# One decoder layer on one core: an eleventh early place for the weights, a fused first-values projection, another token order and a rebuilt end

## The chip, the core and the metric

The kernel runs on one core of a Trainium2 chip. The metric is the device time of one execution in microseconds (us); smaller is better. In the text PE is the matmul engine (TensorE), ScalarE is ACT in the rows, VectorE is DVE, GpSimd is POOL and SyncE is SP; SP issues almost all DMAs. PEld in a row is PE's loading of the stationary operand, which runs beside its matmuls.

## The reference, cut to what matters

One layer of a decoder over 256 tokens of 1024 float32 values: two attention branches (a sliding-window one and a forgetting one) from one input projection, sigmoid gates, an output projection and a layer norm, then a router that picks 4 of 32 experts per token, the experts, and a second layer norm.

```python
proj = h @ w_in[layer]
qa, ka, va, qf, kf, vf, fl, ga, gf = jnp.split(proj, split_points, axis=-1)
...
mix = jax.nn.sigmoid(ga) * ya + jax.nn.sigmoid(gf) * yf
h = _layer_norm(DEEPNORM_ALPHA * h + mix @ w_out[layer], ln1_g[layer], ln1_b[layer])
m = _moe(h, w_router[layer], b_router[layer], w_gate_up[layer], b_gate_up[layer], w_down[layer], b_down[layer])
h = _layer_norm(DEEPNORM_ALPHA * h + m, ln2_g[layer], ln2_b[layer])
```

An expert is `act(xb @ w_gate_up[e]) @ w_down[e]`: 8 MB of weights in its first half and 4 MB in its second, some 400 MB in all, each read once.

## The kernel before, in words

The order of the instructions on each engine is the order of the program: the scheduling is manual, and an engine that waits keeps all that stands behind it waiting. Tiles come from pools with a number of buffers; a new tile of a name takes the buffer of the tile that many allocations before it, and its first writer waits until every reader of that older tile is done. A wait is on semaphores that the framework places.

**The prologue.** The first part computes the input projection in twenty blocks. Each block of `w_in` is loaded by SP, split by `split` (L108 to L111) into a rounded part and a rest (ScalarE writes `hi`, VectorE then writes `lo`), and multiplied with the split, transposed input in three matmuls per chunk: `projT` (L304 to L315) gives transposed results, `projN` (L317 to L330) plain ones. Both write PSUM tiles of the pool `pj`, which has two buffers; `turn_x` uses it too. A block's split stands some blocks ahead of its projection in program order. The first values and forget logits (block 1, 136 columns) go through `projN` at L345, right after the first key projection and the split of block 3; their results leave PSUM through `evac`, which takes ScalarE and VectorE in turn. The attention scores follow, with the remaining blocks in between.

**The middle.** `split_u` (L474 to L492) splits half rows of the two branch projections and of `w_out` for 32 steps u. Steps 5 to 8 and the even ones from 24 have places of their own; all others take a tile `w_r` from five buffers. The splits of steps 0 to 5 stand ahead of the passes that use them. The passes (L570 to L591) run the steps 0 to 12, then 14, 13 and 15; after passes 0 to 4 stand the splits 9 to 13, after the pass of step 9 and every one behind it the splits 14 to 20. Where a pass ends a branch, VectorE multiplies the gate into the result (L582 or L584, L585), ScalarE rounds it (L586) and VectorE forms the rest (L566); the output projection (L614) reads these. The layer norm, the router and the one-hot matrices follow for two halves of 128 tokens, with filler matmuls (`busy`) that keep PE running while VectorE picks the experts (L669 to L680 and the list behind them).

**The weights of the experts.** `load_next` (L142 to L160) loads them in a fixed order, item by item: for each expert the four quarters of its first matrix (2 MB each) and the two halves of its second, which come one expert later. The first 32 items go to small places of 2 MB, a ring of ten that the prologue also uses for its own tiles; an eleventh place, `extra`, is opened after the prologue and used for item 10 alone. From item 32 on, five big places of 4 MB take two items at once. `refill` (L162 to L180) is called after the matmuls that use a place, and lets SP issue the next load; SP waits until the place is free. The first load of the big places follows when the small ones are closed.

**The experts.** Each expert e runs `up_proj` (64 half passes on PE), the combine of expert e-2 into four PSUM accumulators (L900), `scatter`, the gather of later tokens, `swiglu` and `down` of expert e-1. `up_proj` has eight chunks of 128 input channels; a chunk can start when its piece of the weights has landed. Items of the last experts are loaded in pieces: halves from item 166 on, quarters for the three big tiles ahead of the last, and six pieces for the last tile (L129 to L137).

**The end.** `last_down` (L1043 to L1048) runs the last second matrix in two column halves k. `last_combine` (L1050 to L1060) copies a half twice out of PSUM, so that each token half t has it on its own 64 rows, multiplies it into the accumulators and calls `stats`. Then VectorE, ScalarE and GpSimd scale and shift the four quarters (L1071 to L1093), and SP and ScalarE store them.

Of the kernel before, what the change touches and what calls it, by code (L numbers as in the profile page):

```python
# [35 lines left out]
def layer(tc, x, w_in, b_forget, sink, w_proj_swa, w_proj_fox, w_out, ln1_g, ln1_b, w_router, b_router,  # L36
# [9 lines left out]
    with ExitStack() as ctx:  # L46
# [5 lines left out]
        slots = {i: small.enter_context(tc.tile_pool(name=f"slot{i}", bufs=1, side="right")) for i in reversed(slot_of[1:] + slot_of[:1])}  # L52
# [19 lines left out]
        alpha_i = per.tile([P, P], F32, name="alpha_i")  # L72
# [48 lines left out]
        def fetch(kind, e, q, r, n=1, steps=1):  # L121
# [3 lines left out]
            dst, k = r.rearrange("p (c n) -> p c n", c=m * n), m * n // steps  # L125
            for i in range(0, m * n, k):
                sp.dma_start(dst[:, i:i + k], src[:, i:i + k])
# [69 lines left out]
        with tc.tile_pool(name="hd", bufs=1) as hd:  # L197
# [25 lines left out]
            with ExitStack() as at_ctx:  # L223
# [12 lines left out]
                dve.tensor_scalar(alpha_i, ident, ALPHA, None, op0=OP.mult)  # L236
# [45 lines left out]
                def split_in(i, parts=(0, 1)):  # L282
# [3 lines left out]
                    if i not in hls:  # L286
                        tl = slot_tile(1 + i % 3, F32R)
                        hls[i] = [tl[:, 8 * n * k:8 * n * (k + 1)].rearrange("p (c n) -> p c n", n=n) for k in (0, 1)]
                    for q in parts:
                        cs = slice(4 * q, 4 * q + 4)  # L290
                        for k, r in enumerate(raws[i]):
# [5 lines left out]
                            else:  # L297
                                split(*[a[:, cs, 128 * k:128 * k + m] for a in hls[i]], r[:, cs])
# [46 lines left out]
                projN(1, [(v[:, :, 0:128], 0, 128), (fl, 128, 136)])  # L345
# [128 lines left out]
                def split_u(u):  # L474
# [11 lines left out]
                    else:  # L486
                        w_r = p2.tile([P, 2, 512], F32R, name="w_r", bufs=5)
# [5 lines left out]
                for i in range(10):  # L493
# [12 lines left out]
                    if i == 0:  # L506
# [13 lines left out]
                        load_next(2)  # L520
                    if i == 7:
# [33 lines left out]
            wb = hd.tile([P, 8, NE], F32, name="wb")  # L555
            gnat = hd.tile([P, 2, 8], F32, name="gnat")
            sums = hd.tile([P, 2, NE], F32, name="sums")
# [41 lines left out]
            mv = hd.tile([P, 2, 2], F32, name="mv")  # L599
# [69 lines left out]
            def positions(t, pause=None):  # L669
# [3 lines left out]
                if pause:  # L673
                    pause(3)
# [446 lines left out]
```

## Time and profile before

| what | us |
|---|---|
| median of 3 runs | 1119.88 (1118.96 to 1120.91) |
| the profiled execution | 1119.41 |
| its span, first to last instruction | 1117.2 |
| PE busy | 1054.9 (94%) |
| VectorE busy | 378.3 (34%) |
| ScalarE busy | 211.3 (19%) |
| bytes read from HBM | 430.53 MB, 386 GB/s over the span |

The span leaves out what lies around it: the execution took 2.2 us more than its span. A matmul of float32 data shows as two instructions (half passes) in the counts: 64 for the 32 calls of `up_proj`. Busy shares are averages over stages that have different limits; what bounds one stage is read from the waits in it. PE's clock has two levels, 2.4 and 1.2 GHz; a granted clock of 1.00 in a row is the first, 0.50 the second, and what lies between is a mixture over the stretch.

### The profile page before, as it was taken

What the parts mean: (1) busy time and instruction counts of PE and PEld (TensorE: products, weight loads), DVE (VectorE), ACT (ScalarE), POOL (GpSimd) and SP (SyncE); (2) the same over time, 40 slices, a digit from 0 to 9 for tenths busy, and PEclk for the clock granted to TensorE, in tenths of its full rate; (3) what the DMA queues carried; (4) which work ended last, traced back from release to release, by engine and by line L of the source; (5) the groups of instructions that cost most, each with busy time, mean ns of one, the idle gap of its engine ahead of it and who ended that gap; (6) DMA issues with size and microseconds to landing.
All of it is one profiled execution on the core that took longest, in us unless ns stands there. A gap on an engine that the chain in (4) does not pass through costs nothing. (4 is left out here: it accounts for less than half of the span.)

```text
span 1117.2 us, 13432 instructions
## 1 busy us (share of the span) xinstructions
PE 1054.9 (94%) x5677; PEld 517.1 (46%) x5677; DVE 378.3 (34%) x821; ACT 211.3 (19%) x416; POOL 4.8 (0%) x14
## 2 busy tenths in 40 slices
PE   9999999999999999999999999999998988998895
PEld 8988897533333333333333343333433333333322
DVE  5577476432222224222222222222222222222223
ACT  5466464311111110000000110011000000000011
POOL 0000000000000000000000000000000000000001
PEclk9999999999999998999999999999999999999997
DMA  9754599999999999999999999999999999999993
GB/s 274 227 195 146 140 392 354 377 426 405 429 424 429 432 431 416 430 429 430 430 430 431 429 432 431 431 431 430 429 429 431 430 429 430 426 425 428 423 419 121
DMA packets 46406, 432.48 MB, mean 387 GB/s; under 512 B 5524, under 2 KB 26020, under 8 KB 29448
## 3 DMA queue, kind: packets, MB, share of 16 engines
q1 hardware_dynamic: 46144, 431.18, 93.5%
q8 instruction: 46, 0.75, 0.3%
q10 hardware_dynamic: 200, 0.41, 0.1%
q14 instruction: 16, 0.13, 0.0%
HBM read 430.53 MB, written 1.05 MB: 386 GB/s over the span
## 5 line engine op out<-in xcount | busy, mean ns | idle before, releaser
L851 PE MATMUL G<-ww,xTe 128*64 128x512 f32 x1664 | 368.2, 597 | 19.5 <-DMA ww<-in_w_gate_up_dram 19.1
L851 PEld LDWEIGHTS G<-ww,xTe 128*64 128x64 f32 x1664 | 119.3, 138 | 264.1 <-issue 227.3
L886 PE MATMUL X<-ww,aT 128*64 128x512 f32 x864 | 191.3, 595 | 0.5 <-DVE tb L871 0.3
L858 DVE COPY G_sb<-G 128x512 f32<-128x512 f32 x32 | 33.2, 1037 | 408.0 <-PE G L851 408.0
L860 ACT ACTIVATE G_sb<-G 128x512 f32<-128x512 f32 x32 | 33.8, 1055 | 422.3 <-PE G L851 422.3
L886 PEld LDWEIGHTS X<-ww,aT 128*64 128x64 f32 x864 | 59.6, 137 | 113.4 <-issue 107.6
L851 PE MATMUL G<-w,xTe 128*64 128x512 f32 x384 | 83.5, 593 | 0.6 <-POOL nth L773 0.6
L312 PE MATMUL pj<-w 128*128 128x256 f32 x232 | 66.7, 288 | 1.3 <-ACT w L110 0.8
L314 PE MATMUL pj<-w 128*128 128x256 f32 x232 | 65.7, 283 | 0.2 <-DVE w L111 0.2
L313 PE MATMUL pj<-w 128*128 128x256 f32 x232 | 65.6, 283 | 0.0
L809 PE MATMUL X<-OH,h_perm 128*128 128x128 f32 x480 | 63.0, 288 | 1.2 <-DVE h_perm L947 0.9
L900 PE MATMUL acc<-D_sb,GT 64*128 64x512 f32 x248 | 61.6, 615 | 0.7 <-DVE D_sb L893 0.7
L809 PEld LDWEIGHTS X<-OH,h_perm 128*128 128x128 f32 x480 | 60.1, 204 | 1.8 <-PE X L839 1.2
L868 PE MATMUL X<-ident,G_sb 128*128 128x128 f32 x256 | 40.0, 280 | 20.1 <-ACT xTe L822 12.0
L873 ACT ACTIVATE sg<-tb 128x256 f32<-128x256 f32 x64 | 26.7, 416 | 148.5 <-DVE tb L872 148.5
L851 PEld LDWEIGHTS G<-w,xTe 128*64 128x64 f32 x384 | 28.3, 137 | 53.6 <-issue 52.3
L893 DVE COPY D_sb<-X 128x256 f32<-128x256 f32 x31 | 13.2, 425 | 112.0 <-ACT D_sb L892 112.0
L111 DVE TENSOR_TENSOR w<-w 128x1024 fp32r<-128x1024 f32 (+2 forms) x50 | 46.3, 965 | 13.8 <-ACT w L110 13.8
L312 PEld LDWEIGHTS pj<-w 128*128 128x128 f32 x232 | 44.3, 191 | 3.9 <-issue 2.2
L871 DVE TENSOR_TENSOR tb<-X,bT 128x512 f32<-128x512 f32 x64 | 43.7, 683 | 4.1 <-PE X L868 4.1
L314 PEld LDWEIGHTS pj<-w 128*128 128x128 f32 x232 | 44.4, 191 | 0.4 <-DVE w L111 0.4
L313 PEld LDWEIGHTS pj<-w 128*128 128x128 f32 x232 | 44.4, 191 | 0.0
(263 smaller groups left out, 866.6 us busy)
## 6 DMA issues: line engine op xcount, KB each, us to landing
ww<-in_w_gate_up_dram SPq DMA_DIRECT2D x44, 4096.0 KB, 27.2
ww<-in_w_down_dram SPq DMA_DIRECT2D x23, 4096.0 KB, 28.2
w<-in_w_gate_up_dram SPq DMA_DIRECT2D x24, 2048.0 KB, 10.0
ww<-in_w_gate_up_dram SPq DMA_DIRECT2D x12, 2048.0 KB, 38.5
w<-in_w_down_dram SPq DMA_DIRECT2D x8, 2048.0 KB, 10.7
w<-in_w_in_dram SPq DMA_DIRECT2D x14, 1024.0 KB, 5.6
ww<-in_w_down_dram SPq DMA_DIRECT2D x6, 2048.0 KB, 39.7
ww<-in_w_gate_up_dram SPq DMA_DIRECT2D x8, 1024.0 KB, 28.3
```

The source lines that it names most:

```text
L111: dve.tensor_tensor(lo, src, hi.bitcast(F32), op=OP.subtract)
L312: pe.matmul(pt[:, j, :], hi[:, c, cs], xh[:, c, :], start=c == 0, stop=False)
L313: pe.matmul(pt[:, j, :], hi[:, c, cs], xl[:, c, :], start=False, stop=False)
L314: pe.matmul(pt[:, j, :], lo[:, c, cs], xh[:, c, :], start=False, stop=c == 7)
L809: pe.matmul(pt[:, c, :], h_perm[:, t, c0 + c, :], OH[:, t].rearrange("p a s -> p (a s)"), start=t == 0, stop=t == 1)
L851: pe.matmul(G[hf][64 * k:64 * k + 64, :], xT_e[:, c, :], w[:, c % 2, n0:n0 + 512], start=c == 0, stop=c == 7)
L858: dve.tensor_copy(dst, src)
L860: act.activation(dst, src, AF.Copy)
L868: pe.transpose(pt[:, c].rearrange("p k s -> p (k s)"), G_sb[:, c0 + c, :], ident)
L871: dve.tensor_tensor(tb, pt, bias[:, c0:c0 + 4, :, None].to_broadcast([P, 4, 2, CAP]), op=OP.add)
L886: pe.matmul(pt[64 * k:64 * k + 64, :], aT[:, c, :], w[:, c % 4, k * 512:(k + 1) * 512], start=c == 0, stop=c == 7)
L900: pe.matmul(acc[t][k], GT[r, t * P:(t + 1) * P], D_sb[r, :], start=first, stop=False)
```

## The change

It has six parts. The eleventh place is opened at the start, holds item 2 already during the attention (one more `load_next` at its step 3) and stays in the ring until the big places open; for its room the split weights `w_r` get four buffers instead of five, small tiles move from one pool to another, and the scaled identity `alpha_i` is made when it is used. The first values come from one wide matmul per chunk over `hi` and `lo` side by side plus a narrow one, for each token half in a PSUM tile of its own; a ScalarE copy and two VectorE additions sum the parts. In the token tail, the square root moves from `residual` into `shift`, the second half's transposes stand before the first gather, and fewer filler matmuls run. The loads of the experts are whole tiles except for the last three. In the last expert the combine and the scatter run ahead of the last two chunks. The end gets half-width combines, and three of its four output quarters are shifted and scaled by PE: a one-row matmul puts the bias into PSUM, a diagonal matmul adds the scaled values, ScalarE copies the result.

```diff
@@ places
-        slots = {i: ... for i in reversed(slot_of[1:] + slot_of[:1])}
+        slots = {i: ... for i in reversed(slot_of[9:] + slot_of[:9])}
+        extra_ctx = ExitStack()
+        extra = extra_ctx.enter_context(tc.tile_pool(name="extra", bufs=1, side="right"))
+        ring = [*slot_of[:2], None, *slot_of[2:]]
@@ load_next, refill
-                    r = extra.tile([P, 4096], F32, name="w") if i == 10 else slot_tile(slot_of[(i - (i > 10)) % 10])
+                    r = extra.tile([P, 4096], F32, name="w", tag="w") if i % 11 == 2 else slot_tile(ring[i % 11])
...
+                steps = {-6: (1, 1, 2), -4: (1, 1, 1, 1)}
...
-                    fetch(kind, slice(e, e + 1), q, r, 2, 4 if i + 8 >= len(items) else 2 if i + 26 >= len(items) else 1)
+                    fetch(kind, slice(e, e + 1), q, r, 2, *steps.get(i - len(items), (1,)))
...
-                if i - (11 if i < 21 else 10) >= used[0] - keep:
+                if i - (11 if nxt[0] < SMALL else 10) >= used[0] - keep:
@@ first values
-                projN(1, [(v[:, :, 0:128], 0, 128), (fl, 128, 136)])
+                for t in range(2):
+                    pt = pjp.tile([P, 2, 136], F32, name="pj")
+                    ts = slice(t * P, (t + 1) * P)
+                    for c in range(8):
+                        w = hls[1][2][:, c].rearrange("p k n -> p (k n)")
+                        pe.matmul(pt.rearrange("p k n -> p (k n)"), xh[:, c, ts], w, start=c == 0, stop=False)
+                        pe.matmul(pt[:, 0], xl[:, c, ts], hls[1][0][:, c, :], start=False, stop=c == 7)
+                    vl = at.tile([P, 136], F32, name="vl")
+                    act.activation(vl, pt[:, 1], AF.Copy)
+                    dve.tensor_tensor(v[:, t, 0:128], pt[:, 0, :128], vl[:, :128], op=OP.add)
+                    dve.tensor_tensor(fl[:, t], pt[:, 0, 128:], vl[:, 128:], op=OP.add)
@@ split weights, the extra load
-                        w_r = p2.tile([P, 2, 512], F32R, name="w_r", bufs=5)
+                        w_r = p2.tile([P, 2, 512], F32R, name="w_r", bufs=4)
...
+                    if i == 3:
+                        load_next()
@@ tokens
-                    act.activation(rs[:, t:t + 1], mv[:, t, 1:2], AF.Sqrt, bias=eps)
...
             def shift(t):
+                act.activation(rs[:, t:t + 1], mv[:, t, 1:2], AF.Sqrt, bias=eps)
...
-                    pause(3)
+                    pause(1)
...
+            shift(0)
             turn(0, 0, act)
             turn(0, 1, act)
-            shift(0)
...
-            gather0(0, 0)
             turn(1, 1, act)
             shift(1)
+            gather0(0, 0)
...
-            busy(idle, 2)
+            busy(idle, 1)
...
-            load_next()
@@ last expert
             def up_proj(xT_e, weights, beside=None):
...
+                    if c == 6 and beside:
+                        beside()
...
+                def others():
+                    if e > 1 and e != OVER + 1:
+                        combine(GTs[e - 2], Ds[e - 2], e == 2)
+                    if e == last:
+                        GTs[e] = scatter(OHg)
+                G_sb = up_proj(xTs[g][:, :, e % 2, :], lambda kind, q: where[kind, e, q], others if e == last else None)
                 refill(4, 2 if e == OVER else 0)
+                if e < last:
+                    others()
@@ end
             def last_combine(k):
...
+                for j in range(2):
+                    src, c = pt[k][64 * j:64 * j + 64], slice(256 * j, 256 * j + 256)
+                    act.activation(D2[:64, c], src, AF.Copy)
+                    dve.tensor_copy(D2[64:, c], src)
+                    for t in range(2):
+                        r = slice(64 * t, 64 * t + 64)
+                        pe.matmul(acc[t][k][:, c], GTs[last][r, t * P:(t + 1) * P], D2[r, c], start=False, stop=j > 0)
...
             last_down(1, 6, 7)
-            last_combine(0)
             last_down(1, 7, 8)
-            last_combine(1)
+            for k in range(2):
+                last_combine(k)
+                if k == 0:
+                    for t in range(2):
+                        stats(t, 0)
+            base = {}
+            for t, k in ((0, 0), (0, 1), (1, 0)):
+                base[t, k] = xp.tile([P, 512], F32, name="X") if t else gp.tile([P, 512], F32, name="G")
+                pe.matmul(base[t, k], ones[NE:NE + 1, :], rows[NE:NE + 1, cs[k]], start=True, stop=False)
...
+            def inverse(t):
+                dve.reciprocal(rs[:, t:t + 1], rs[:, t:t + 1])
+                diag[t] = mo.tile([P, P], F32, name="sg", bufs=2)
+                dve.tensor_scalar(diag[t], ident, rs[:, t:t + 1], None, op0=OP.mult)
+            def by_pe(t, k):
+                pe.matmul(base[t, k], diag[t], shifted[:, t, cs[k]], start=False, stop=True)
+                act.activation(y[:, t, cs[k]], base[t, k], AF.Copy)
+                store(t, k)
+            stats(0, 1)
+            scaled(0, 0)
+            inverse(0)
+            by_pe(0, 0)
+            stats(1, 1)
+            scaled(0, 1)
+            by_pe(0, 1)
+            inverse(1)
+            scaled(1, 0)
+            by_pe(1, 0)
+            scaled(1, 1)
+            dve.scalar_tensor_tensor(y[:, 1, cs[1]], shifted[:, 1, cs[1]], rs[:, 1:2], gb[:, 1, cs[1]],
+                                     op0=OP.mult, op1=OP.add)
+            store(1, 1)
```

`stats(t, k)` is one statistics operation on VectorE; for k = 1 an aggregation and ScalarE's square root follow. `scaled(t, k)` subtracts the mean and multiplies by the gain on VectorE, and `store` is an SP DMA. The four stores, and the loop of the last combine that is taken out, are left out of the diff above.

## Rows read from the trace of the kernel before

**Rows 1.** Windows: stretch, its length, PE, PEld, DVE, ACT, POOL, PEclk, DMA, GB/s.
```profile
269.00:272.00 3.00, 3.00 (x18) 1.00 (x16) 0.04 (x1) 0.00 (x0) 0.00 (x0) 1.00 0.76 240
272.00:430.00 158.00, 149.80 (x734) 58.33 (x730) 42.24 (x93) 19.30 (x37) 0.00 (x0) 1.00 1.01 429
810.00:960.00 150.00, 137.11 (x666) 52.57 (x662) 35.68 (x77) 13.27 (x25) 0.00 (x0) 0.98 1.00 430
965.00:1055.00 90.00, 83.79 (x416) 32.40 (x412) 22.39 (x47) 9.26 (x17) 0.00 (x0) 1.00 1.00 426
1060.00:1090.00 30.00, 27.27 (x126) 8.67 (x122) 6.43 (x15) 4.14 (x7) 0.00 (x0) 1.00 1.01 419
```
**Rows 2.** Timeline of SP, 194 to 205: start, length, instruction, count.
```profile
194.69 9.70 SPq L127 DMA_DIRECT2D w<-in_w_gate_up_dram  x2
```
**Rows 3.** Timelines of ACT, PE and DVE in the first 30 us.
```profile
12.16 0.23 PE L325 MATMUL pj<-w 128*128 128x136 f32 x1
...
17.48 0.33 PE L312 MATMUL pj<-w 128*128 128x256 f32 x1
...
29.80 0.36 PE L312 MATMUL pj<-w 128*128 128x256 f32 x1 [0.47 <-DVE w L97]
...
16.09 0.36 ACT L93 ACTIVATE w<-pj 128x256 f32<-128x256 f32 x1
...
20.15 1.67 ACT L110 ACTIVATE w<-w 128x512 fp32r<-128x512 f32 x3 [1.74 <-DMA w<-in_w_in_dram]
...
22.63 0.42 DVE L95 COPY v<-pj 128x256 f32<-128x256 f32 x1
```
**Rows 4.** Windows again, columns as in rows 1: two stretches at half clock.
```profile
661.00:664.40 3.40, 3.08 (x15) 2.91 (x14) 0.00 (x0) 0.71 (x2) 0.00 (x0) 0.51 1.03 443
1104.80:1117.00 12.20, 2.24 (x3) 0.50 (x2) 7.75 (x14) 1.37 (x3) 2.85 (x2) 0.50 0.23 86
```
**Rows 5.** Timelines of ACT, DVE and PE, 148 to 169, around the split weights.
```profile
152.55 0.63 ACT L110 ACTIVATE w_r<-w 128x512 fp32r<-128x512 f32 x1 [1.22 <-PE X L578]
...
156.75 0.63 ACT L110 ACTIVATE w_r<-w 128x512 fp32r<-128x512 f32 x1 [0.77 <-PE G L578]
...
158.02 0.68 DVE L584 TENSOR_TENSOR w<-w,G 128x512 f32<-128x512 f32 x1
...
167.75 0.50 PE L614 MATMUL acc<-w_r,w 128*128 128x512 f32 x1 [0.59 <-ACT w_r L110]
```
**Rows 6.** Timelines of PE and ACT, 189 to 201: the last tokens.
```profile
191.19 1.14 PE L684 MATMUL X<-OH,h_perm 128*128 128x128 f32 x8
...
193.52 1.08 PE L658 MATMUL acc<-wr,hT 128*128 128x32 f32 x8 [0.75 <-ACT hT L647]
...
197.75 2.02 PE L684 MATMUL X<-OH,h_perm 128*128 128x128 f32 x16 [0.17 <-DVE OH L679]
...
194.88 2.31 ACT L634 ACTIVATE h_perm<-x_sb,nm,rs 128x512 f32<-128x512 f32 x2
```
**Rows 7.** The chain that ended last, from the last expert's last chunk.
```profile
1078.52 1.94 PE G L851 x8
1080.46 1.92 PE acc L900 x8
...
1095.06 4.49 PE X L1047 x40
...
1104.10 2.96 PE acc L1058 x4
...
1113.41 0.75 DVE ww L1078
```
**Rows 8.** The page's costliest groups: busy us, mean ns, idle before.
```profile
L851 PE MATMUL G<-ww,xTe 128*64 128x512 f32 x1664 | 368.2, 597 | 19.5 <-DMA ww<-in_w_gate_up_dram 19.1
...
L858 DVE COPY G_sb<-G 128x512 f32<-128x512 f32 x32 | 33.2, 1037 | 408.0 <-PE G L851 408.0
```
**Rows 9.** Timeline of PE, 657 to 661: one-row matmuls.
```profile
657.02 3.79 PE L936 MATMUL X<-rows,ones 1*128 1x512 f32 x8
```

More of the change, by code (lines that the diff above doesn't have):

```diff
@@ L119, in layer, with fetch @@
         where, nxt, used, big = {}, [0], [0], []
-        def fetch(kind, e, q, r, n=1, steps=1):
+        def fetch(kind, e, q, r, n=1, *parts):
             src, m = (w_gate_up, 2) if kind == "G" else (w_down, 4)
             src = src[e].rearrange("a (p c) n -> p (a c) n", c=8)[:, m * q:m * q + m * n, :]
-            dst, k = r.rearrange("p (c n) -> p c n", c=m * n), m * n // steps
-            for i in range(0, m * n, k):
-                sp.dma_start(dst[:, i:i + k], src[:, i:i + k])
+            dst, i, unit = r.rearrange("p (c n) -> p c n", c=m * n), 0, m * n // max(sum(parts), 1)
+            for k in parts or (1,):
+                sp.dma_start(dst[:, i:i + k * unit], src[:, i:i + k * unit])
+                i += k * unit
         def fetch_last(r):
@@ L297, in split_in @@
                             else:
-                                split(*[a[:, cs, 128 * k:128 * k + m] for a in hls[i]], r[:, cs])
+                                split(*[a[:, cs, 128 * k:128 * k + m] for a in hls[i][:2]], r[:, cs])
                     if 1 in parts and i != 11:
@@ L970, in layer @@
                     OH = onehot(g + 1)
-                G_sb = up_proj(xTs[g][:, :, e % 2, :], lambda kind, q: where[kind, e, q])
+                def others():
[4 more added lines that the diff above has]
+                G_sb = up_proj(xTs[g][:, :, e % 2, :], lambda kind, q: where[kind, e, q], others if e == last else None)
                 refill(4, 2 if e == OVER else 0)
-                if e > 1 and e != OVER + 1:
-                    combine(GTs[e - 2], Ds[e - 2], e == 2)
+                if e < last:
+                    others()
                 if e == NORM:
@@ L1001, in layer @@
                     act.dma_start(rows[NE:], ln2_b)
-                GTs[e] = scatter(OHg)
+                if e < last:
+                    GTs[e] = scatter(OHg)
                 if 2 * (g + 1) <= last:
@@ L1052, in last_combine, with stats, scaled, store @@
                 D2 = mo.tile([P, 512], F32, name="tb", bufs=2)
-                for r in (slice(0, 64), slice(64, P)):
-                    act.activation(D2[r, :256], pt[k][:64], AF.Copy)
-                    dve.tensor_copy(D2[r, 256:], pt[k][64:])
-                for t in range(2):
-                    r = slice(64 * t, 64 * t + 64)
-                    pe.matmul(acc[t][k], GTs[last][r, t * P:(t + 1) * P], D2[r], start=False, stop=True)
-                for t in range(2):
-                    stats(t, k)
+                for j in range(2):
[5 more added lines that the diff above has]
+                        pe.matmul(acc[t][k][:, c], GTs[last][r, t * P:(t + 1) * P], D2[r, c], start=False, stop=j > 0)
+            def stats(t, k):
+                dve.bn_stats(stt[:, t, k], acc[t][k])
+                if k == 1:
+                    dve.bn_aggr(mv[:, t], stt[:, t])
+                    act.activation(rs[:, t:t + 1], mv[:, t, 1:2], AF.Sqrt, bias=eps)
+            def scaled(t, k):
+                dve.scalar_tensor_tensor(shifted[:, t, cs[k]], acc[t][k], mv[:, t, 0:1], gb[:, 0, cs[k]],
+                                         op0=OP.subtract, op1=OP.mult)
+            def store(t, k):
+                sp.dma_start(out[t * P:(t + 1) * P, cs[k]], y[:, t, cs[k]])
             for c in (0, 2, 4):
@@ L1090, in layer @@
-            for k in range(2):
-                scaled(1, k)
-                shifted(1, k)
-            act.dma_start(out[0:P, cs[1]], y[:, 0, cs[1]])
+            for k in range(2):
[7 more added lines that the diff above has]
+                pe.matmul(base[t, k], ones[NE:NE + 1, :], rows[NE:NE + 1, cs[k]], start=True, stop=False)
@@ new lines, in layer @@
+            diag = {}
+            def inverse(t):
[7 more added lines that the diff above has]
+            stats(0, 1)
```

61 lines of the change are left out of this document (22 added, 39 removed).

## The prediction

> **What bounds the kernel now.** I read the busy time by windows first. From 272 us on the 16 DMA engines are never idle and move 429 to 430 GB/s in whole tiles [rows 1], while PE is busy 137 us of 150 (810 to 960) and waits for weights: the end is set by the DMA queue, and by when that queue became full. The reader is to see two exceptions. From 269 to 272 the share falls to 0.76: there the queue had nothing it was allowed to load. And the queue is full only from about 204, because before that all eleven places hold weights and PE has not yet freed the first. The issue timeline shows it: the eleventh place is loaded from 194.69, the next load is the second of that row, whose issue ends the row at 204.39 [rows 2]. So the end moves with the moment at which PE begins the first expert, not with how early a place is filled. The stretch before that is PE's (its timeline has hardly a gap), then one of VectorE and ScalarE. The last 40 us are read from the chain of waits.
>
> **First values.** Before, 48 matmuls run from 12.16 to 17.48, and the next projection follows at once [rows 3]. After, 16 of 272 columns and 16 of 136; from the spacing of 0.11 (5.32 / 48) and, for 272, about 0.12, that is 3.7 us, 1.6 less. But now each token half takes a PSUM tile of its own, of two. That such a tile holds PE is visible: at 29.80 a projection waits 0.47 us for VectorE to empty the tile two before it. The second half therefore needs the tile of the first projection, which ScalarE empties at 16.09 to 16.45, behind the splits; and the third projection needs the tile of the first half, which is emptied by a ScalarE copy and two VectorE additions. These stand behind the splits of the fourth block, which wait for their DMA and end on ScalarE at 20.15 + 1.67 = 21.82, on VectorE where its copy starts now, 22.63. So the third projection starts near 23.2 instead of 17.48. The two projections take 11.6 us (17.48 to 29.1); the next starts at 34.8 instead of 29.80 (the 0.47 goes): **+5.0 us**. Everything behind it on PE shifts, to the attention's end; the new operations of VectorE lie in PE's wait. PE then idles 2.4 and 4.8 us; after waits the granted clock falls, and a fall as in 661.0 to 664.4 (0.51 over 3.4 us [rows 4]) costs at most 1.7, at least nothing. I take **+1.3**, since most of it would meet running matmuls. Bounds: -1.6 if the tile held nobody, +6.7.
>
> **Four buffers for the split weights instead of five.** With five, the split of pass 14 waits for pass 9 on PE to end (152.55), that of 17 for pass 12 (156.75) [rows 5]; a pass is 1.40 us. With four, each waits for one further on: 13 for pass 9 (152.55), 14 for 10, 15 for 11, 16 for 12, and 17 for pass 13, which PE runs after 14: 156.7 + 2 x 1.4 = 159.5. Queued behind split 17 on VectorE stand the gate products that begin at 158.02 now, and after them all that the output projection reads. After: ScalarE 159.6 to 160.2, VectorE's half 0.68, products at 160.9: **+2.9 us**. VectorE is then busy without a gap until PE waits for it and ScalarE (0.59 at 167.75), so nothing absorbs it. The early wait of split 4 (0.8 us on ScalarE) is covered by passes PE already has. Bounds 0 and 3.2.
>
> **Order of the last tokens.** PE's transposes for the second half now run before the first gather (1.14 at 191.19), so the logits that wait 0.75 at 193.52 start 0.6 earlier [rows 6]. Three filler matmuls fewer stand in the way of the positions, and the gather at 197.75, which waited for VectorE's one-hot, comes when ScalarE's h is ready, 197.19 less 0.5. **-1.0**, bounds 0 and -1.2. The square root moved behind the copy on ScalarE has slack.
>
> **Eleventh place.** Loading it near 92 us instead of 194.69 uses idle DMA time, but at the first expert both kernels hold eleven filled places, so it gives nothing there. What it gives: the eleventh place stays until the big tiles, so the stop at 269 goes: 3 x (430 - 240) / 430 = **-1.3**. Moving the small tiles and the scaled identity costs nothing: VectorE has idle time beside PE's matmuls; without that cover 0.3.
>
> **Pieces.** Halves moved 426 GB/s, quarters 419, whole tiles 430 [rows 1]: nine tiles of 4.19 MB at 430 instead of 426 save 0.8, the tile of the last expert's first half 0.3: **-1.0** rounded.
>
> **Last expert on PE.** Its first half now lands as one piece. At 4.19 MB and 419 GB/s that is 10 us before the row at 1078.52 [rows 7], 1068.5. From then PE has eight chunks, 1.77 each (368.2 us / 1664 x 8) [rows 8]; the moved combine (1.92) and a 0.3 scatter stand before the last two. Ends: 1068.5 + 8 x 1.77 + 2.2 = 1084.9; the copy out of PSUM (1.04), which the combine hid at 1080.46, is bare: the transposes start at 1086.0, against 1082.5 now (1078.52 + 1.94 + 1.92 + 0.1). PE then has work without a gap until its last down projection, so **+3.3** less 0.2 for coarser starts: **+3.1**. Bounds 0.8 (PE only loses the bare copy) and 4.8 (a low clock at 1068.5).
>
> **After the last matmul.** Without the wait for the first combine, all down projections would now end at 1095.06 + 4.49 + 0.5 + 0.3 = 1100.4; from there to the end it is 16.8 us. After: copies and half-width matmuls end the second combine at +4.8 instead of +6.7 (1104.10 + 2.96). But then three one-row matmuls go ahead, 0.95 each at the full clock (eight half passes took 3.79 [rows 9]) and 1.9 at half, before the first 128-row one (the same again); the second token half's square root is queued on ScalarE behind the copy of the first result, and with it reciprocal, diagonal, product, two more matmuls and a copy. Full clock: 4.8 + 2.9 + 0.95 + 0.65 + 0.9 + 0.7 + 0.95 + 0.65 = 12.5; half clock: 9.9 (the fall comes at some point near +4.6) + 6.7 = 16.6; then a second store (0.35) and what follows VectorE's last operation now (1113.41 + 0.75 to 1117.2, 3.05). That is 15.9 or 20.0. The clock in this stretch is 0.50 already now, from 1104.8, with PE idle for most of it, and PE has less to do after: I take 20.0, **+3.2**; bounds -0.9 and +4.3.
>
> Eight one-row matmuls back to back (657.02 to 660.8 [rows 9]) did not hold the clock: it is 0.51 right after [rows 4]. The Trainium skill ("TensorE: Matmul & The Clock Gate", part 1, "What's actually happening") says that the clock follows how busy PE has been and that activity releases the throttle; by that the one-row matmuls would keep it at 2.4 GHz and the sum would be 4.1 us smaller. The trace doesn't bear this out for one-row matmuls.
>
> **Sum.** 5.0 + 1.3 + 2.9 - 1.0 - 1.3 - 1.0 + 3.1 + 3.2 = +12.2. The profiled execution took 1119.4 (span 1117.2 and 2.2 around it), 0.5 under the median of the three runs; against the median it gives 1132.1, rounded 1132.
>
> **Rivals.** (1) No buffer holds anybody: PE gets its PSUM tile and the splits their buffer in time. Place: the start of the third projection; it decides if ScalarE's and VectorE's readings of the tile end before 17.5. Price: -1.6 instead of +6.3, and 0 instead of 2.9, so -10.8: 1121, not slower by what can be told. Against it stand the waits at 29.80 and 152.55, which are of this kind; for it, that the first columns might be read earlier. (2) The end at full clock, as the busy PE would have it: -4.1, 1128. For it: PE does run matmuls there; against it, 661.0. (3) Only one of the two buffers holds: 1129 without the split's, 1124 without PSUM's. (4) More time at the low clock, at the early idle, at 1068.5 and in the middle of the prologue: +1.7 each, two of them 1136. (5) The end set by DMA after all, PE catching up: 3.1 becomes 0.8, 1130.
>
> **Chances.** Forecast 0.5 (1130 to 1134), rival 1 0.1, rival 2 0.12, 3 0.1, 4 0.1, 5 0.08. A range of 1124 to 1138 leaves out rival 1 and, with the bounds of the single terms, little on top. What can be told from no change is about 0.2%, 2.2 us. Rival 1 with the lower bounds of the last two terms spreads from 1115 to 1123: of its 0.1 I give 0.06 to faster and 0.04 to the same; slower has 0.9.
>
> **What would show it.** Right: PE idle near 14 and from 18 to 23 in the prologue; the third projection at 23; ScalarE's split 17 waiting for PE until 159.5 plus the shift; the first expert 8 us later; no dip where 269 was; PE running the last expert without waiting on DMA, 5 us behind the last landing; one-row matmuls of 1.9 us. Wrong: a third projection at 16, or a first expert no later than now; then the buffers don't hold and the forecast is about 10 us too high. If the first expert comes 8 us later but the end does not move, the queue was not the bound.

## The result: 1.1% slower, as forecast, and the profile after

| what | before | after |
|---|---|---|
| median, us | 1119.48 (4 runs, 1118.96 to 1120.91) | 1132.54 (4 runs, 1130.28 to 1133.51) |
| ratio to before | | 1.0110, 95% interval 1.0095 to 1.0125 |
| the profiled execution, its span | 1119.41, 1117.2 | 1132.52, 1130.7 |
| PE busy | 1054.9 | 1067.3 |

The forecast was 1132.0 with a range of 1124 to 1138. The same moments in the two traces show where the 13.5 us of span come from:

| moment | before | after | shift | forecast |
|---|---|---|---|---|
| third projection starts [rows 3] | 17.48 | 23.41 | +5.9 | +5.7 |
| ScalarE's split 13 [rows 5] | 152.55 | 161.41 | +8.9 | +6.3 |
| ScalarE's split 17 [rows 5] | 156.75 | 167.31 | +10.6 | +9.2 |
| last gather [rows 6] | 197.75 | 207.06 | +9.3 | +8.2 |
| SP may go on behind the eleven filled places [rows 2] | 204.39 | 213.73 | +9.3 | +8.2 |
| end of the last down matmul, 1100.4 without the wait for the first combine | 1100.4 | 1112.17 | +11.8 | +9.0 |
| last instruction | 1117.2 | 1130.7 | +13.5 | +12.2 |

Of the 13.5 us, 9.3 are there before the first expert begins. Two lines of the kernel before, PE at the attention's transposes and at the first expert:

```profile
63.96 0.44 PE L456 MATMUL tp<-ident,S 128*128 128x128 f32 x2 [0.58 <-ACT w L457]
...
200.38 1.08 PE L851 MATMUL G<-w,xTe 128*64 128x512 f32 x4 [0.61 <-POOL nth L773]
```

PE's timeline of the changed kernel, from 17 to 24 (the rows that answer to [rows 3]), and further down, at the attention's transposes, the branch projections, the output projection, the last gather and the first expert:

```profile
17.75 0.40 PE L358 MATMUL pj<-w 128*128 128x272 f32 x1 [3.41 <-ACT w L95]
...
23.41 0.55 PE L319 MATMUL pj<-w 128*128 128x256 f32 x1 [3.02 <-DVE fl L363]
...
71.71 0.55 PE L474 MATMUL tp<-ident,S 128*128 128x128 f32 x3 [0.58 <-ACT w L475]
...
146.23 0.39 PE L596 MATMUL acc<-w,w_r 128*128 128x256 f32 x1 [1.17 <-ACT w_r L112]
...
178.31 0.50 PE L634 MATMUL acc<-w_r,w 128*128 128x512 f32 x1 [0.64 <-ACT w_r L112]
...
207.06 0.60 PE L704 MATMUL X<-OH,h_perm 128*128 128x128 f32 x3 [0.27 <-ACT h_perm L654]
...
209.72 1.04 PE L870 MATMUL G<-w,xTe 128*64 128x512 f32 x3 [0.61 <-POOL nth L790]
```

Read the brackets: the second token half waits 3.41 us for ScalarE to copy the first key projection out of its PSUM tile, and the third projection 3.02 us for VectorE's last sum to empty the tile of the first half. Each names an engine that reads a tile, not one that makes data for PE: a wait for room.

ScalarE's timeline, 160 to 170, of the splits (answers to [rows 5]), and SP's around the first expert (answers to [rows 2]):

```profile
161.41 0.63 ACT L112 ACTIVATE w_r<-w 128x512 fp32r<-128x512 f32 x1 [1.15 <-PE X L598]
...
165.73 0.63 ACT L112 ACTIVATE w_r<-w 128x512 fp32r<-128x512 f32 x1 [0.81 <-PE G L598]
167.31 0.63 ACT L112 ACTIVATE w_r<-w 128x512 fp32r<-128x512 f32 x1 [0.94 <-PE G L598]
```
```profile
200.99 12.74 SPq L129 DMA_DIRECT2D w<-in_w_gate_up_dram  x2
```

The windows of the changed kernel, columns as in [rows 1]: the clock in the prologue, the place where the dip of [rows 1] stood, and the last 18 us:

```profile
16.00:20.00 4.00, 2.25 (x15) 2.26 (x16) 2.46 (x4) 2.32 (x5) 0.00 (x0) 0.89 1.14 301
20.00:24.00 4.00, 0.98 (x5) 0.80 (x5) 2.60 (x8) 2.12 (x5) 0.00 (x0) 0.50 1.08 350
24.00:28.00 4.00, 4.00 (x20) 4.00 (x20) 2.65 (x17) 3.46 (x5) 0.00 (x0) 0.50 0.93 284
28.00:32.00 4.00, 4.00 (x31) 4.00 (x30) 2.17 (x2) 0.15 (x1) 0.00 (x0) 0.83 0.14 28
278.00:281.00 3.00, 3.00 (x16) 1.01 (x14) 0.39 (x1) 0.00 (x0) 0.00 (x0) 1.00 1.02 431
...
1112.00:1118.00 6.00, 4.63 (x21) 2.63 (x20) 4.20 (x9) 1.43 (x4) 0.00 (x0) 1.00 0.00 0
1118.00:1125.00 7.00, 6.66 (x9) 1.89 (x7) 3.35 (x10) 1.20 (x3) 0.00 (x0) 0.51 0.09 35
```

The dip is gone (431 GB/s where 240 stood). In the prologue PE comes out of its second wait at half clock and stays there to about 29.4 (the 0.83 of the last four us), working without a gap; the clock had fallen near 19.1, during the second token half (the 0.89 of the first four us). The end, from the chain that ended last (answers to [rows 7]):

```profile
1033.87 42.82 DMA ww<-in_w_gate_up_dram
1076.73 10.52 PE G L870 x48
1087.25 1.92 PE acc L919 x8
...
1106.84 5.33 PE X L1071 x48
1112.17 1.25 PE acc L1083 x6
...
1116.81 2.31 PE G L1115 x4
1119.12 1.71 PE X L1115 x2
1120.83 2.02 PE G L1124 x2
...
1122.87 0.60 ACT ww L1125
...
1124.88 1.20 PE X L1124 x2
```

The DMA hands over to PE at 1076.73 and never comes back into the chain: from there PE works through the last expert and both second matrices, 35.4 us to 1112.17, while the last landing is at 1106.67. PE's own timeline shows how long it had waited for expert 30 and for the last expert:

```profile
1057.26 1.12 PE L870 MATMUL G<-ww,xTe 128*64 128x512 f32 x2 [3.99 <-DMA ww<-in_w_gate_up_dram]
...
1076.73 0.65 PE L870 MATMUL G<-ww,xTe 128*64 128x512 f32 x2 [0.36 <-DMA ww<-in_w_gate_up_dram]
```

The three one-row matmuls (L1115) take 4.0 us and the first diagonal one (L1124) 2.0.

### The profile page after: what moved, and what is told of

The parts are those of the page before. It is cut to its first block, busy times and chain, and to the rows that moved or that the text cites. A ratio compares the mean times of both kernels' runs of the same rounds, so it can differ in the third digit from the quotient of the medians.

```text
span 1130.7 us, 13416 instructions
## 1 busy us (share of the span) xinstructions
PE 1067.3 (94%) x5675; PEld 524.7 (46%) x5675; DVE 377.4 (33%) x824; ACT 213.0 (19%) x419; POOL 2.0 (0%) x12
## 3 DMA queue, kind: packets, MB, share of 16 engines
HBM read 430.53 MB, written 1.05 MB: 382 GB/s over the span
## 5 line engine op out<-in xcount | busy, mean ns | idle before, releaser
L319 PE MATMUL pj<-w 128*128 128x256 f32 x232 | 67.9, 293 | 4.0 <-DVE fl L363 3.0
L321 PE MATMUL pj<-w 128*128 128x256 f32 x232 | 66.9, 288 | 0.2 <-DVE w L113 0.2
L320 PE MATMUL pj<-w 128*128 128x256 f32 x232 | 66.8, 288 | 0.0
L319 PEld LDWEIGHTS pj<-w 128*128 128x128 f32 x232 | 45.7, 197 | 6.5 <-issue 5.4
L321 PEld LDWEIGHTS pj<-w 128*128 128x128 f32 x232 | 45.7, 197 | 0.4 <-DVE w L113 0.4
L320 PEld LDWEIGHTS pj<-w 128*128 128x128 f32 x232 | 45.7, 197 | 0.0
```

The lines of the kernel that those rows point to most:

```text
L319: pe.matmul(pt[:, j, :], hi[:, c, cs], xh[:, c, :], start=c == 0, stop=False)
L320: pe.matmul(pt[:, j, :], hi[:, c, cs], xl[:, c, :], start=False, stop=False)
L321: pe.matmul(pt[:, j, :], lo[:, c, cs], xh[:, c, :], start=False, stop=c == 7)
```

## The experiments

Two parts of the change blur what is read behind them: the prologue's half clock differs from execution to execution, and the queue carries a shift to the end. So some runs alter the changed kernel itself, others stand on its version with the old first values, whose prologue is that of the kernel before; each says which. Times are medians of all runs of a kernel; ratios are to the kernel before, measured beside it.

**Old first values.** `split_in` and the loop of the first values as before:

```diff
-                for t in range(2):
-                    pt = pjp.tile([P, 2, 136], F32, name="pj")
...
+                projN(1, [(v[:, :, 0:128], 0, 128), (fl, 128, 136)])
```

> The changed kernel with the first values computed as before (48 narrow matmuls, both token halves in one PSUM tile, copies instead of sums); all else stays. Theory, PSUM tile holds PE: the third projection starts near 17.5 us instead of 23.41, the half-clock stretch of 19.11 to 29.35 goes, every later step comes 7.8 to 8.7 us earlier, and the end with them, since from the first expert on the DMA queue is full: 1124 to 1125 us. Rival, the prologue is late because the eleventh place's load or the shorter ring of split buffers delays it, and PE's idle time at 14 and 20 us is absorbed later: the third projection still moves to 17.5, but the first expert moves by less than 3 us, and the time is 1129.5 or more.

Measured: 1126.2 us, ratio 1.0055 (1.0033 to 1.0076). First expert:

```profile
201.01 0.65 PE L857 MATMUL G<-w,xTe 128*64 128x512 f32 x2 [0.61 <-POOL nth L777]
```

That is 8.7 us earlier than 209.72, the upper end of what was expected, so the rival's absorption is out, and the wait at the branch projections is gone with it. The time moved by 6.3 instead of 7.5 to 8.5: the tail behind the last down matmul was 20.4 us in this trace against 18.55.

**The halves in a free PSUM tile.** One line:

```diff
-                    pt = pjp.tile([P, 2, 136], F32, name="pj")
+                    pt = scp.tile([P, 384], F32, name="sc")[:, :272].rearrange("p (k n) -> p k n", k=2)
```

> The changed kernel with only the two PSUM tiles of the first values taken from another pool, whose buffers nobody else needs at that time (three buffers, one used by the filler); the fused matmuls stay. Theory, it is the tile and not the fused arithmetic that costs: PE goes from the first key projection through both halves without a wait and starts the third projection at 16.0 to 16.6 us, 1 us or more ahead of the kernel before; whether that 1 us survives depends on the split of the fourth block, which ends near 22.6 and on which the fourth projection waits, so the first expert is 8.6 to 9.5 us earlier than in the changed kernel and the time 1123 to 1124 us. Rival, the two sums on VectorE behind the splits hold the chain as such: third projection at 16, but the fourth or fifth projection waits 3 us or more, and the time is 1127 or more.

Measured: 1129.69 us, 1.0080 (1.0048 to 1.0112). The expectation fell; the rival came nearer. PE's and VectorE's timelines of this run:

```profile
17.19 0.39 PE L319 MATMUL pj<-w 128*128 128x256 f32 x1 [0.86 <-ACT w L112]
...
31.62 0.36 PE L319 MATMUL pj<-w 128*128 128x256 f32 x1 [2.19 <-DVE w L99]
```
```profile
24.62 0.15 DVE L363 TENSOR_TENSOR fl<-sc,vl 128x8 f32<-128x8 f32 x1
...
28.52 2.36 DVE L113 TENSOR_TENSOR w<-w 128x1024 fp32r<-128x1024 f32 x2 [0.21 <-issue]
30.80 0.68 DVE L99 TENSOR_SCALAR w<-pj 128x512 f32<-128x512 f32 x1
```

Both halves run without a wait, but the third projection then waits for its own split and starts at 17.19, only 0.3 earlier than in the kernel before: what the fused matmuls save has nowhere to go. And the second sum ends on VectorE at 24.77. Behind it stand the forget gates and two splits, and only then the copy that empties a projection's tile, at 30.80; PE waits 2.19 us for it where it waited 0.47 [rows 3]. So PSUM's tiles explain the waits of 3.41 and 3.02, but freeing them does not make the fusion pay: it puts its sums on an engine that was nearly late already. At the attention's transposes this run is 1.8 us behind the kernel before (65.77); at the first expert (205.65) it is 4.6 us behind the version with the old first values. The rest comes at the branch projections, where PE waits 1.54 us and then works at half clock from 142.5 to 145.9.

**Filler in the waits.** In the loop over the token halves, behind the sums:

```diff
                     dve.tensor_tensor(fl[:, t], pt[:, 0, 128:], vl[:, 128:], op=OP.add)
+                    busy(idle, 13)
```

> The changed kernel with 13 filler matmuls (about 2.9 us at the full clock) behind each token half of the first values, in the two waits of PE; nothing else. Theory, the two waits cost twice, once as waits and once because the clock is halved when PE comes out of them: with the filler the granted clock stays at 1.00 from 12 to 32 us, the third projection starts near 23.4 as in the changed kernel, but everything behind it is 3 us earlier: first expert 206.7, 1129.5 us. Rival, the filler only takes the place of the waits and the clock falls all the same, or falls later: 1131.5 us or more.

Measured: 1130.86 us, 1.0102 (1.0086 to 1.0118); the profiled execution took 1128.22. Its windows and the third projection:

```profile
20.00:24.00 4.00, 2.77 (x25) 2.61 (x25) 2.44 (x7) 2.12 (x5) 0.00 (x0) 1.00 1.09 348
24.00:28.00 4.00, 4.00 (x36) 4.00 (x35) 2.65 (x18) 3.43 (x5) 0.00 (x0) 1.00 0.95 298
28.00:32.00 4.00, 4.00 (x35) 4.00 (x35) 4.00 (x5) 2.19 (x3) 0.00 (x0) 1.00 0.10 22
```
```profile
23.44 0.35 PE L319 MATMUL pj<-w 128*128 128x256 f32 x1 [1.23 <-DVE fl L363]
...
69.12 0.44 PE L475 MATMUL tp<-ident,S 128*128 128x128 f32 x2 [0.58 <-ACT w L476]
```

The third projection starts where it did (23.41), the clock stays at 1.00, and the attention's transposes come at 69.12 instead of 71.71: the half clock costs 2.6 us in the same code with the same waits. The first expert came 3.8 us earlier (205.96), 0.7 more than expected: PE does not wait at the branch projections here (0.00 instead of 1.17). The medians differ by 1.7 us and their intervals overlap, so the gain is shown by one trace and not by the times: the other four executions had mean clocks of 0.977 to 0.980 against the traced one's 0.982, and whether the filler held the clock in them is not shown.

**Four split buffers alone,** in the kernel before:

```diff
-                        w_r = p2.tile([P, 2, 512], F32R, name="w_r", bufs=5)
+                        w_r = p2.tile([P, 2, 512], F32R, name="w_r", bufs=4)
```

> The kernel before with four buffers for the split weights instead of five, and nothing else. Theory, the split of step 17 gets the first buffer that a pass frees (step 14's, one pass after that of step 16) and so starts 1.8 us later, and what VectorE forms behind it too; the first expert moves from 200.38 to 202.2 and the end with it: 1121.3 us. Rival, the forecast's: split 17 waits for step 13's pass, 2.9 us: 1122.4 us. Rival, the shift is absorbed in PE's waits at the output projection: 1119.5 us.

Measured: 1121.25 us, 1.0011 (0.9999 to 1.0022). ScalarE's split 17 and the first expert:

```profile
156.91 0.63 ACT L110 ACTIVATE w_r<-w 128x512 fp32r<-128x512 f32 x1 [0.77 <-PE G L578]
158.59 0.63 ACT L110 ACTIVATE w_r<-w 128x512 fp32r<-128x512 f32 x1 [1.05 <-PE G L578]
```
```profile
202.25 0.65 PE L851 MATMUL G<-w,xTe 128*64 128x512 f32 x2 [0.61 <-POOL nth L773]
```

The first expert moves by 1.87 us. The median moves by 2.0, but the interval includes no change, and the traced execution, with its first expert 1.87 later, was no longer than the kernel before (span 1117.0 against 1117.2): that the end moved is not shown. The split follows that of step 16 by 1.68 us, one pass, not two, and it waits for a G tile, which pass 14 writes (pass 13 writes X).

**The old token order,** on the version with the old first values (the hunk on the tokens taken back, of which two places stand here):

```diff
-                    pause(1)
+                    pause(3)
...
+            gather0(0, 0)
             turn(1, 1, act)
             shift(1)
-            gather0(0, 0)
```

> The changed kernel with the old first values and the old order of the last tokens (square root right behind the statistics, first gather ahead of the second half's transposes, three more filler matmuls). Theory, the new order is worth 1.2 us: the first expert moves from 201.0 to 202.2 and the time from 1126.2 to 1127.4 us. Rival, worth nothing: first expert at 201.0.

Measured: 1125.7 us, 1.0056 (1.0039 to 1.0072). The time did not rise: it is within what 1126.2 varies by (1124.77 to 1127.57). In the trace the first expert is at 201.85, 40.07 us behind the first matmul of the output projection instead of 39.02: by the traces the new order is worth 1.05 us, and the times cannot show it.

**Quarters for the last expert,** in the changed kernel and then on the old first values:

```diff
-                steps = {-6: (1, 1, 2), -4: (1, 1, 1, 1)}
+                steps = {-8: (1, 1, 1, 1), -6: (1, 1, 1, 1), -4: (1, 1, 1, 1)}
```

> The changed kernel with the last expert's first matrix loaded in quarters of 1 MB throughout (its first 4 MB came whole, its second as two quarters and a half); combine and scatter stay ahead of the last two chunks. Theory, PE's arrears at the end are the chunks that stand after the landing of whole pieces: PE follows the pieces, ends the last chunk near 1088.5 instead of 1093.2 and the last down matmul near 1107.7, 1 us behind the last landing: 4.3 less, 1128.2 us. Rival, the arrears come from the moved combine and scatter (2.3) alone and from the low clock: the last chunk ends at 1091 or later, 1130.5 us or more.

> The changed kernel with the old first values (the experiment that gave 1126.2) and, on top, the last expert's first matrix in quarters of 1 MB. The first expert stays near 201.0 and the last landing near 1099, so that the end alone differs. Theory, PE follows the pieces: the last chunk begins 3.4 us earlier than 1084.33 and the last down matmul ends near 1100.5 instead of 1103.96: 1122.8 us. Rival, PE's arrears don't come from whole pieces: less than 1 us earlier, 1125.5 us or more.

Measured: 1132.58 us, 1.0115 (1.0087 to 1.0143), and 1122.95 us, 1.0028 (1.0014 to 1.0043). The first shows nothing: its first expert came 1.4 us later (211.12; PE waited 1.87 at the branch projections and then worked at half clock from 148.1 to 151.4) and its queue was 2.4 us later at the end (425 million bytes, counted from the DMA packets, are in at 1089.1 against 1086.7), which eats what the end may have won. The second has the expected time, but not by the expected path. In its chain:

```profile
1008.13 38.71 DMA ww<-in_w_gate_up_dram
1046.88 8.78 PE G L857 x32
...
1066.26 10.30 PE G L857 x48
```

PE starts the last expert at 1066.26, and not for a landing: it has been working without a gap since 1046.88, when the second half of expert 30's first matrix landed, whole too. So the arrears begin one expert earlier (in the changed kernel too: it waits 3.99 us for the same piece and, at the last expert, 0.36), and 1.9 us of the difference to 1126.2 lie ahead of it, in a queue that was that much earlier in this execution (the same count: 1078.1 against 1080.0). Quarters for the last expert alone are worth little; that they explain the 3.3 us is not shown.

**The old end,** in the changed kernel and then on the old first values (the whole hunk on the end taken back):

```diff
-            free = big_tile()
...
+            y = big_tile()[:, :2 * D].rearrange("p (t n) -> p t n", t=2)
...
+            last_combine(0)
+            last_down(1, 7, 8)
+            last_combine(1)
...
-            store(1, 1)
...
+            act.dma_start(out[0:P, cs[1]], y[:, 0, cs[1]])
```

> The changed kernel with the end as before (combine in two whole halves, the scaling and shifting on VectorE, ScalarE and GpSimd, no one-row and no diagonal matmuls); all else stays. Theory, the new end takes longer from PE's last down matmul on: 16.8 us from there to the last instruction instead of 18.5, so 1130.8 us. Rival, the new end is as quick or quicker and only the later last down matmul shows: 1132.5 or more.

> The changed kernel with the old first values and the old end. Theory, from the first matmul of the last second matrix to the last instruction the old end takes 26.6 us (26.1 in the kernel before), the new one 29.9 with its half clock from about 4 us behind the last down matmul: 3.3 less, 1122.9 us. Rival, the new end is slow only by its place behind a late PE: less than 1 us, 1125.5 us or more.

Measured: 1129.23 us, 1.0082 (1.0059 to 1.0106), 3.3 less; and 1121.2 us, 1.0020 (1.0010 to 1.0030), 5.0 less. Both moved more than expected. From the first matmul of the last second matrix the old end takes 26.6 and 25.7 us, the new one 28.05 in the changed kernel and 29.9 on the old first values. So by the traces the end itself is worth 1.4 and 4.2 us; the other 1.9 and 1.3 us by which these executions were shorter lie ahead of it. The windows of the latter show why it is not the same twice:

```profile
1104.00:1110.00 6.00, 4.63 (x17) 2.56 (x18) 3.91 (x9) 1.44 (x4) 0.00 (x0) 0.81 0.00 0
1110.00:1118.00 8.00, 8.00 (x10) 2.50 (x8) 2.72 (x9) 0.78 (x2) 0.00 (x0) 0.50 0.00 0
```

There the clock falls about 3.7 us behind the last down matmul (1103.96), ahead of all three one-row matmuls; in the changed kernel 6 us behind its 1112.17, while the second of them runs.

**One-row matmuls ahead.** Old first values, old pieces, the new end with two of its one-row matmuls ahead of the last down matmuls:

```diff
                     combine(GTs[last - 1], Ds[last - 1])
+                    for n in range(2):
+                        pe.matmul(base[0, n], ones[NE:NE + 1, :], rows[NE:NE + 1, cs[n]], start=True, stop=False)
...
-            for t, k in ((0, 0), (0, 1), (1, 0)):
+            for t, k in ((1, 0),):
```

> The changed kernel with the old first values, the old pieces and the new end, of whose three one-row matmuls two stand right behind the last combine ahead of the last down matmuls. Theory, the tail of 20.4 us is long because one-row matmuls of 1.85 us at half clock stand ahead of everything that PE still has to do: two of them (3.7 us) leave the tail and lie in PE's waits: tail 16.7 us, last down matmul as in the combined version: 1118.4 us. Rival, what holds the end is the second square root and its chain behind the first result, not PE: tail 19 us or more, 1120.5 us or more.

Measured: 1121.09 us, 1.0013 (1.0004 to 1.0021). The tail is 16.5 us, as expected; the time is not, because PE did not wait where they were put:

```profile
1094.72 1.92 PE acc L906 x8
1096.64 1.91 PE G L1092 x4
1098.55 5.33 PE X L1058 x48
```

They stand in the chain at full clock, 1.9 us. Moving them saves half of their price, not all. The last down matmul ends at 1103.88, 4.1 us behind the combined version below; the other 2.2 us are there when the last second matrix begins (1092.67 against 1090.46), as the queue was that much later (425 million bytes at 1081.4 against 1079.1).

**The combined version.** Old first values, old pieces, half-width combines with the old scaling:

```diff
             for k in range(2):
                 last_combine(k)
-                if k == 0:
-                    for t in range(2):
-                        stats(t, 0)
...
-            stats(0, 1)
+            for t in range(2):
+                for k in range(2):
+                    stats(t, k)
```

> The changed kernel with three parts taken back: the first values as before, the pieces of the last experts as before (halves, and quarters for the three tiles ahead of the last), and behind the half-width combines the old scaling and shifting, with both combines ahead of all statistics on VectorE. Kept: the eleventh place with four split buffers, the token order, the combine ahead of the last two chunks. Theory, the arrears of PE come from whole pieces of the last two experts, not from the last one alone: PE waits for pieces to the end and its last down matmul ends within 3 us of the last landing (about 1097.2 and 1099.5), and the tail takes 14.8 us from there (4.6 for the combines, 10.2 for the old scaling) instead of 20.4: span 1114, 1116.2 us, faster than the kernel before. Rival, the arrears stay (5 us behind the last landing): 1118.5 or more.

Measured: 1115.94 us, ratio 0.9967 (0.9955 to 0.9979): faster than both kernels. PE waits for the last experts' pieces again, and the chain at the end:

```profile
1042.66 0.65 PE L857 MATMUL G<-ww,xTe 128*64 128x512 f32 x2 [1.26 <-DMA ww<-in_w_gate_up_dram]
...
1068.07 0.65 PE L857 MATMUL G<-ww,xTe 128*64 128x512 f32 x2 [1.12 <-DMA ww<-in_w_gate_up_dram]
...
1072.91 0.65 PE L857 MATMUL G<-ww,xTe 128*64 128x512 f32 x2 [0.56 <-DMA ww<-in_w_gate_up_dram]
```
```profile
1094.43 4.49 PE X L1058 x40
...
1102.07 1.31 DVE stt L1073 x2
...
1105.43 0.75 DVE ww L1093
```

The last down matmul ends at 1099.76, 4.2 us earlier than with whole pieces, and the tail is 13.8 us: from 1102.07 on it is VectorE's, and PE's clock no longer matters.

**Two parts alone on the kernel before:** the token order, and the same end.

> The kernel before with two parts of the change alone: the order of the last tokens, and half-width combines behind all down matmuls, with the old scaling and shifting. Theory: first expert 1.2 us earlier (199.2), the last down matmul ends at 1099.2 because it no longer waits for the first combine, 14.8 us of tail: span 1114.0, 1116.2 us. Rival, the DMA queue was not moved by the first expert: first expert 199.2 but the last landing at 1098.6 as before, 1117.4 us.

Measured: 1116.32 us, 0.9968 (0.9955 to 0.9981). Without the eleventh place it is as fast as with it, so the place, its four split buffers and the moved combine together are worth nothing that the times can tell; that the buffers cost what the place brings is a reading of this, not a test. The profiled execution was the longest of seven, 1119.79: PE worked at half clock between 11 and 14.6 us (0.53), and the transposes came at 65.05. From the first matmul of the output projection to the first expert it took 38.59 us where the kernel before took 39.63, the 1.04 of the token order, and its tail is 13.8 us as in the combined version.

## Why the prediction was right, point by point

The sum was +12.2 and came out at +13.5. That the times agree to less than 1 us is in part luck: five of the seven terms missed by 0.9 to 1.5 us each, three upwards and two downwards, and the last one differs by up to 2 us between traces of the same end.

| term | forecast | measured |
|---|---|---|
| first values and low clock | +6.3 | +7.75 (63.96 to 71.71) |
| wait at the branch projections | 0 | +0.9 (0.23 before, 1.17 after) |
| four split buffers | +2.9 | +1.9 (alone, at the first expert) |
| order of the last tokens | -1.0 | -1.05 (in the pair that differs by it alone) |
| eleventh place and pieces | -2.3 | -1.2 at the landing that PE waits for (1068.51 to 1076.69) |
| last expert on PE | +3.1 | +3.6 |
| after the last matmul | +3.2 | +1.7 here, +3.6 with a 20.4 us tail |

- **First values:** the mechanism held to 0.2 us: both halves wait for tiles in the order foretold, third projection at 23.41 against 23.2. The waits came as 3.41 and 3.02 where 2.4 and 4.8 were foretold: ScalarE's splits ahead of the first copy ended at 17.43 instead of 16.18, since their DMA landed later; the next splits, ahead of the sums, began only 0.3 later (20.44 against 20.15). The term mis-sized was the low clock, taken as a fall like that of [rows 4]: "I take +1.3, since most of it would meet running matmuls". PE ran at half clock from 23.41 to about 29.4, which is 3.0 us lost, and the filler run gives 2.6 for it. The size of this term differs between executions: the same code in the run with the old end shows clocks of 0.80 and 0.77 where the changed kernel has 0.50 and 0.50.
- **A lower bound that was none:** "-1.6 if the tile held nobody" was rival 1's price. The free tile showed +1.8 at the attention's transposes, since the next split isn't ready and VectorE becomes late.
- **Split buffers:** the step that failed is "17 for pass 13, which PE runs after 14". Split 17 waited for the pass of step 14, which ended first: one pass (1.6 us with its wait), not two.
- **The branch projections** had no term. Their first split waits for the second transfer of `w_proj_swa`, which took 13.5 us from issue to landing (131.68 to 145.16) against 12.6 before. With the eleventh place but the old first values it took 12.5, so it isn't that load; in the two runs with the longest waits there (1.54 and 1.87) it took 13.9 and 14.2, and with the filler, where nothing waits, 12.3. Why stays open. In those two runs half clock followed the wait, so this missing term can be larger than 0.9.
- **Eleventh place:** counted from the DMA packets, the shift against before falls from 9.45 us at 70 million bytes to 7.96 at 80 million: the dip gave 1.5, a little more than 1.3. All traces agree: the three with the old use of the place take 24.8 to 25.3 us for this stretch, the eleven with the new one 23.3 to 23.4. **Pieces:** from 350 to 425 million bytes it falls from 8.0 to 6.9, near the 1.0 foretold (whose parts, 0.8 and 0.3, make 1.1; five traces with the old pieces take 175.1 to 175.3 us, nine with whole ones 173.9 to 174.6). But the whole tile that PE waits for lands 8.18 us later than the quarter that ended at the same byte before: what larger pieces gained in rate they lost in the landing of the whole.
- **Last expert:** right in size: from 1076.73 to 1093.15 the eight chunks with the combine and the scatter take 16.4 us, as forecast. (The prediction's 1086.0 less 1082.5 is 3.5, where it says 3.3; the term measured 3.6.) But PE had waited only 0.36 us for that landing and had worked since 1057.26, so the cause lies one expert further back than "From then PE has eight chunks" says: expert 30's halves are whole as well, and pieces for the last expert alone could have won 0.4. The combined version, with all old pieces, ends the last down matmul 4.2 us earlier than the version with the old first values (1099.76 against 1103.96); 0.9 of it is its earlier queue (425 million bytes at 1079.1 against 1080.0), which leaves 3.3 for the pieces.
- **Tail:** 20.0 was foretold, with the fall "near +4.6" (its 9.9 at half clock is 10.5 by its own terms, 4.8 and three times 1.9; on the old first values the third one-row matmul ends at +10.6). Of the six other traces with this end unaltered, four show 20.2 to 20.4 (the one shown above with the fall at +3.7) and two 18.3 and 18.8, like the changed kernel's 18.55 with the fall at +6. Rival 2, the full clock, is out: in 1118 to 1125 PE was busy 6.66 of 7.00 us at 0.51. The rule of the Trainium skill named there ("TensorE: Matmul & The Clock Gate", part 1, "What's actually happening"), by which activity releases the throttle, does not agree with this trace.

- **The other rivals:** 1 and 3 are out, since both buffers hold; 5 is out, since DMA ends nothing behind 1076.73; 4 happened at its first place, the early idle, and the end was still inside the forecast's own 1130 to 1134 because the tail and the split's wait were shorter.

The first reason of all, that the end moves with the first expert, holds for the large shifts: the old first values moved the first expert by 8.7 us and the last landing by 7.5, the filler the first expert by 3.8 and the 425 millionth byte by 3.9. For a shift of 1 or 2 us no trace can show it, since from the first expert to that byte the fourteen traces take between 876.8 and 881.4 us: with four buffers alone the first expert came 1.87 later and that byte 0.9, with the old token order the first expert came 0.84 later and that byte 0.95 earlier.

## What to carry to other kernels

A shorter sequence of matmuls is worth what the next thing PE needs is early: here the next block's split was ready 0.3 us before, so a saving of 1.6 us was paid with a second PSUM tile, sums on a nearly late engine and half a clock. When a kernel is bound by a queue that is full from some moment on, look for what delays that moment, and at the end for work that stands behind the landing of a large piece; the size that is best for the queue's rate is not the best for the engine that waits. Take a change of many parts apart before it is dropped: two of its parts made the kernel 0.3% faster.

## What the runs showed of the hardware

- The granted clock does not come back at once when PE works again: 23.41 to about 29.4 without a gap at 0.5 in the changed kernel. In all three traces with these two waits and no filler it fell during the second token half or the wait behind it; in the one with filler it stayed at 1.00.
- PE can be busy all the time and remain at half clock: 8.00 of 8.00 us at 0.50 in 1110 to 1118 of the run with the old first values, with one-row matmuls and the first diagonal one in it.
